# A decoder layer on one core: attention steps in another order, the last expert by hand, unread products

## The chip, the core and the metric

The kernel runs on one core of a Trainium2 chip. TensorE (PE) multiplies; its granted clock has two levels, 2.4 GHz (1.00 in the rows) and 1.2 GHz (0.50). VectorE (DVE), ScalarE (ACT) and GpSimd (POOL) work element by element; SyncE (SP) starts the loads of weights, one after the other. Sixteen DMA engines move the data. The metric is the device time of one launch in microseconds (us), the median of several runs. All times here are us unless marked ns.

## The reference

A decoder layer for S=256 tokens of D=1024, everything fp32: a condition c gives six vectors (shift, scale, gate, twice); attention with 16 heads of 64 (eight with compressed, selected and window branches, eight with a sliding window and a sink); a gated merge; an output projection; then 32 experts, of which each token uses four.

```python
mod = (cond @ w_ada + b_ada)                       # sh1, sc1, ga1, sh2, sc2, ga2
h = rms_norm(x, g_mix) * (1 + sc1) + sh1
q_n, kv_n, gate_n, q_s, kv_s, gate_m = split(h @ w_in)
o_n = nsa_attention(q_n, compress(k_c), compress(v_c), k_sl, v_sl, k_w, v_w, sigmoid(gate_n), rel_tab)
o_s = swa_attention(q_s, k_s, v_s, sinks, rel_tab)
g_a, g_b = split(sigmoid(gate_m))
x = x + ga1 * ((g_a * (o_n @ w_branch[0]) + g_b * (o_s @ w_branch[1])) @ w_out)
h = rms_norm(x, g_ffn) * (1 + sc2) + sh2
logits = h @ w_router + b_router                   # top 4 of 32, softmax over the four
for e in range(32):                                # each for the tokens that chose it
    y += gate_e * (clamped_swiglu(h @ w_up[e] + b_up[e]) @ w_down[e] + b_down[e])
return rms_norm(x + ga2 * y, g_final)
```

## The kernel before

**Weights.** All large weights come in chunks of 1 MB by `chunk()` (L197), which issues a load on SP's queue into one of 18 named slots (`ALL`), and into a nineteenth that the merge leaves. SP issues in program order: a load whose slot is not free holds up all behind it, and eight loads are under way at most. An expert is 12 chunks: 8 of `wup`, 4 of `wdn`. In the front of the program the same slots hold the chunks of w_ada, w_in, w_branch and w_out; as these are used up, the first chunks of experts 0 and 1 are loaded into them ahead of need.

**Front.** Products with fp32 weights are three products of a high and a low part: ACT casts the high part (L266), DVE subtracts for the low part (L271), and PE runs hh, hl and lh (L494 to L496, L990 to L992). `split` does both casts. The order of PE, DVE and ACT in the attention is written out by hand: classes `s0`, `s1` (sliding window) and `n0`, `n1` (the other eight heads) have steps `scores` (PE, then DVE L572 or L621 for bias and maximum, then ACT for the exponential L624), `weigh` (DVE and ACT L550, L552, each half of the heads times 1/sum), `turn` (PE transposes L538, ACT copies L540), `values` (PE L546) and `close` (ACT L523, DVE L524). `hidden` is the first layer of the compression (L771); its sum `hx` (L792) leaves its PSUM bank, for which the next piece of the merge gates waits. Between the steps `fill()` puts one piece of the merge gates on PE. After it come the branch products, `projected(q, f)` (w_out), and for each quarter q of the columns `added(q)` (residual), `turned(q)` (transposes, squares) and `logits(q)` (L1037).

**Choice of experts.** `fold` (L1077) adds the four partial logits, DVE finds the four best (L1080 to L1087), `pp` (L1090 to L1094) counts positions with products of 0/1 matrices, `oh` (L1139) is the one-hot matrix of expert 0's tokens. `gather` takes the norms of these tokens (L1129, fp32 products) and their rows in eight groups of 128 features (L1151, high and low part), DVE and ACT scale them to `XT` (L1153, L1154). Expert 0 starts with `z<-chunk,XT` (L1196): its first two columns of `XT` go through two banks each, so its first chunk is free after eight products.

**Last expert.** Its `wdn` is stored apart (`wlast`), four chunks of 256 columns each, the last in two parts of 0.5 MB. For each, PE multiplies (L1419), DVE scales (L1422), ACT and DVE split (L1427, L1428), PE spreads the rows back to the tokens (L1430, L1431), DVE adds to `y` (L1437), ACT squares (L1440). Then the last norm (L1444, L247) and the output in two halves of 512 columns for each 128 tokens (L1448 to L1451). The scheduler orders these engines.

Of the kernel before, what the change touches and what calls it, by code (L numbers as in the profile page):

```python
# [10 lines left out]
F32 = mybir.dt.float32  # L11
# [70 lines left out]
def _layout(inp):  # L82
# [40 lines left out]
    wl = wd[E - 1].reshape(2, 4, 128, 4, 256).transpose(3, 2, 1, 0, 4)  # L123
    tail = wl[3].reshape(128, 4, 2, 2, 128).transpose(0, 3, 1, 2, 4)
    out["wlast"] = c(np.concatenate([wl[:3].reshape(3, 128, 2048), tail.reshape(1, 128, 2048)]))
# [36 lines left out]
def tile_trunk(ctx: ExitStack, tc: tile.TileContext, A, out: bass.AP, dbg=None):  # L162
# [49 lines left out]
    count = fixed([1, E + 1], I32, "count")  # L212
    most = fixed([1, 1], F32, "most")
# [39 lines left out]
    with tc.tile_pool(name="front", bufs=1) as fr, tc.tile_pool(name="banks", bufs=1, space=PSUM) as ps:  # L253
# [54 lines left out]
        with tc.manual_schedule(engines=by_hand):  # L308
# [37 lines left out]
            ACT.copy(rrow, pr)  # L346

# [206 lines left out]
        class Sliding:  # L554
# [22 lines left out]
            def weigh(self):  # L577
                sm = self.sm
                V.tensor_tensor(sm[:, 2], sm[:, 0], C("sinks"), op=OP.add)
                ACT.activation(sm[:, 2], sm[:, 2], AF.Exp)  # L580
                V.tensor_tensor(sm[:, 1], sm[:, 1], sm[:, 2], op=OP.add)
                V.reciprocal(sm[:, 1], sm[:, 1])
                for i in range(4):
# [105 lines left out]
        with tc.manual_schedule(engines=by_hand):  # L689
# [24 lines left out]
            def compress(kv):  # L714
                kx = fr.tile([128, 2, S], F32, name="kx", tag="PT", bufs=4)
                for l2 in range(2):
                    for g in range(2):
                        eng = V.tensor_copy if g else ACT.copy
                        eng(kx[l2 * 64:l2 * 64 + 64, g, 0:S - l2], zb[0][g * 64:g * 64 + 64, kv, l2:S])
                b = bls[:, kv]  # L720
# [77 lines left out]
            ACT.activation(hu, hx, AF.Square)  # L798
            fill()
# [37 lines left out]
            n0.sums()  # L837
            n1.scores(0)
            n0.weigh(0)
# [16 lines left out]
            n0.values(1, pT)  # L856
            n1.scores(3)
            n0.compressed_turn()
# [31 lines left out]
            def branch_halves():  # L890
                for h in range(2):
                    for b in (1, 0):
                        w = chunk(A["wbr"], 2 * h + b).rearrange("p (f n) -> p f n", f=2)
                        for f in range(2):
                            yield split(w[:, f], 1024)
                ws = []
                for q, f in ((0, 0), (1, 0), (0, 1), (1, 1), (2, 0), (2, 1), (3, 0), (3, 1)):
                    if f == 0:
                        ws.append(chunk(A["wout"], q).rearrange("p (f n) -> p f n", f=2))
                    yield split(ws[q][:, f], 1024)  # L900
# [3 lines left out]
            nxt = next(ready)  # L904
            fill()

# [14 lines left out]
            for h in range(2):  # L921
                t = gm[h]
                for b in (1, 0):
                    pz = [bank(x, [128, 512]) for x in ("zo", "zz")[b]]
                    for f in range(2):
                        wh, wl = nxt
                        for i2 in range(2):
# [7 lines left out]
                            if i2 == 0:  # L935
                                nxt = next(ready)
                            elif f == 0:
                                next(passing)
# [35 lines left out]
            r2 = fixed([128, 2], F32, "r2")  # L974
            pl = bank("two", [128, S])
# [4 lines left out]
            def projected(q, f):  # L980
                wh, wl = nxt
                if f == 0:
                    pzs[q] = bank("z", [128, 2, 256])
                pz = pzs[q]
                for k4 in range(4):
# [7 lines left out]
                    if k4 == 1:  # L993
                        following = next(ready, None)
# [17 lines left out]
            def turned(q):  # L1012
                t, pt = tails[q]
                cs = slice(q * 256, q * 256 + 256)
                for d1 in range(2):
                    for a in range(2):
                        dk = 2 * q + d1
                        PE.transpose(pt[:, d1, a, :], xt[:, a, dk * 128:(dk + 1) * 128], ident)
                for k in range(2 * q, 2 * q + 2):
                    V.tensor_scalar(wr2[:, k], wr[:, k], G2[:, k:k + 1], None, op0=OP.mult)  # L1020
                for a in range(2):
                    ACT.activation(t[:, a], xt[:, a, cs], AF.Square, accum_out=ss[:, a, q:q + 1])
                if q == 3:
                    V.tensor_copy(x1T[:, 2 * q:2 * q + 2].rearrange("p a b -> p (a b)"), pt.rearrange("p a b c -> p (a b c)"))
                    V.tensor_reduce(s2, ss, X, OP.add)
                    V.tensor_scalar(s2, s2, 1.0 / D, 1e-5, op0=OP.mult, op1=OP.add)
                    root = POOL.tensor_tensor(r2, s2, half, op=OP.pow).ins
                else:
                    ACT.copy(x1T[:, 2 * q:2 * q + 2].rearrange("p a b -> p (a b)"), pt.rearrange("p a b c -> p (a b c)"))
# [9 lines left out]
            nxt = projected(0, 0)  # L1039
            merge_turn(1, 0)  # L1040
            next(passing)
            nxt = projected(1, 0)
            merge_turn(1, 1)
            nxt = projected(0, 1)
            next(passing)
            added(0)
            nxt = projected(1, 1)
            next(passing)
            added(1)
            turned(0)  # L1050
            nxt = projected(2, 0)
# [3 lines left out]
            nxt = projected(2, 1)  # L1055
# [5 lines left out]
            nxt = projected(3, 0)  # L1061
# [5 lines left out]
            logits(2)  # L1067
            added(3)
            turned(3)
            logits(3)  # L1070

# [22 lines left out]
        PE.matmul(pp[:, 2], ones, mask[:, 1], start=False, stop=True)  # L1094
        V.scalar_tensor_tensor(posm, pp[:, 0:2], 1.0, mask, op0=OP.add, op1=OP.mult)
        for name, t in (("d_x1", xt), ("d_lg", lg), ("d_posm", posm), ("d_gates", gates)):
# [19 lines left out]
    with tc.tile_pool(name="moe", bufs=1) as mo, tc.tile_pool(name="banks2", bufs=1, space=PSUM) as ps:  # L1116
# [7 lines left out]
        def norms(oh):  # L1124
# [3 lines left out]
            for a in range(2):  # L1128
                PE.matmul(p, r2[:, a:a + 1].to_broadcast([128, 128]), oh[:, a].bitcast(F32), start=a == 0, stop=a == 1)  # L1129
# [55 lines left out]
        def up(e, XT, c0, step=lambda j: None):  # L1185
# [3 lines left out]
            for n in range(2):  # L1189
                for j in range(4):  # L1190
                    if n == 0:
                        step(j)
                    w = chunk(A["wup"], e * 8 + 4 * n + j, slots=ALL).rearrange("p (k c f) -> p k c f", k=2, c=2)
                    for k in range(2):
                        for c in range(2):
                            PE.matmul(gu[n][64 * c:64 * c + 64], XT[:, 2 * j + k, c0:c0 + 64], w[:, k, c],  # L1196
                                      start=j == 0 and k == 0, stop=False)
                PE.matmul(gu[n], chosen[e % 2], bias[:, n * 512:(n + 1) * 512], start=False, stop=True)  # L1198
# [157 lines left out]
        with tc.issue_after(first[1]):  # L1356
            V.tensor_copy(count[:, 0:E], pp[0:1, 2])
            V.tensor_reduce(most, pp[0:1, 2], X, OP.max)
# [10 lines left out]
        for e in range(E):  # L1369
# [17 lines left out]
            if e == E - 1:  # L1387
                hT_ = [act(gu, n) for n in range(2)]
# [18 lines left out]
        ss = mo.tile([128, 2, 5], F32, name="ss3", tag="rr")  # L1407
        banks = pair("po") + pair("gu")
        for j in range(4):
            w = chunk(A["wlast"], j, slots=ALL, parts=1 + j // 3).rearrange("p (h b c n) -> p h c b n", h=1 + j // 3,  # L1410
                                                                             c=2, b=4)
            for h in range(1 + j // 3):
                n = 256 >> j // 3
                i = j + h
                cs = slice(j * 256 + h * n, j * 256 + h * n + n)
                po = (bank("pt", [128, 512]) if h else banks[j])[:, 0:n]
                for b in range(4):
                    for c in range(2):
                        PE.matmul(po[64 * c:64 * c + 64], hT_[b // 2][:, b % 2, 64 * c:64 * c + 64], w[:, h, c, b],  # L1419
                                  start=b == 0, stop=b == 3)  # L1420
                t = mo.tile([128, n], F32, name="t", tag="th", bufs=2)
                V.tensor_tensor(t, po, g2b[:, cs], op=OP.mult)  # L1422
                p = bank("s", [128, 2, 256])
                if j < 3:
                    hi = mo.tile([128, n], F32R, name="ohi")
                    lo = mo.tile([128, n], F32R, name="olo")
                    ACT.copy(hi, t)  # L1427
                    V.tensor_tensor(lo, t, hi.bitcast(F32), op=OP.subtract)  # L1428
                    for a in range(2):
                        PE.matmul(p[:, a], r[:, a], hi, start=a == 0, stop=False)  # L1430
                        PE.matmul(p[:, a], r[:, a], lo, start=False, stop=a == 1)  # L1431
                else:
                    p = [p[:, 0, 0:n], bank("s", [128, n])]
                    for a in range(2):
                        PE.matmul(p[a], r[:, a].bitcast(F32), t, start=True, stop=True)
                for a in range(2):
                    V.scalar_tensor_tensor(y[:, a, cs], p[a] if j == 3 else p[:, a], gates[:, a, E - 1:E], y[:, a, cs],  # L1437
                                           op0=OP.mult, op1=OP.add)
                    sq = mo.tile([128, n], F32, name="sq", tag="li")
                    ACT.activation(sq, y[:, a, cs], AF.Square, accum_out=ss[:, a, i:i + 1])  # L1440
                (V if h else POOL).tensor_tensor(last[:, :, cs], y[:, :, cs],
# [28 lines left out]
```

## Time and profile before

| what | value |
|---|---|
| median of 3 runs | 1182.69 (1178.37 to 1182.98) |
| profiled execution | 1183.18, of which 2.0 lie outside the span of 1181.2 |
| PE busy | 94% of the span |
| DVE, ACT busy | 43%, 23% |
| DMA | 463.61 MB, 392 GB/s in the mean |
| mean granted clock of PE | 0.977 |

Busy times are sums over the whole program. PE's share holds products that run while the weights of a later expert are still on their way, so a high share alone does not say that PE sets the end. A release "<-" in a row names what an engine's idle time ended with.

### The profile page before, as it was taken

To read this page: it belongs to the slowest core of one execution; us is meant where nothing else is said; L and a number is where in the kernel's file an instruction comes from. 1 tells how busy PE (TensorE), PEld (TensorE's weight loads), DVE (VectorE), ACT (ScalarE), POOL (GpSimd) and SP (SyncE) were. 2 spreads that over 40 slices of the span, in tenths; PEclk is the share of its full clock that TensorE was granted. 3 is DMA by queue.
4 is the path that set the end of the run, shared out by engine and by line. 5 is a ranking of instruction groups with operands and counts; after the bars stand their busy time and mean duration, and the time that the engine had idled before them with its cause. 6 is when DMAs were issued, how large, how long until landed. Compare 5 with 4: busy or idle time off the path is not lost. (4 is left out here: it accounts for less than half of the span.)

```text
span 1181.2 us, 13548 instructions
## 1 busy us (share of the span) xinstructions
PE 1106.8 (94%) x5209; PEld 488.8 (41%) x5210; DVE 513.3 (43%) x1067; ACT 266.1 (23%) x618; POOL 28.1 (2%) x25
## 2 busy tenths in 40 slices
PE   7998999899998999899999969999999999999996
PEld 6965678633342333223333324333333333333323
DVE  6877779623344323423343332333332333243333
ACT  4657734311120112111211112112111211121102
POOL 0000000100000000400000000000000000000001
PEclk9999999899999999999999989999999999999998
DMA  9986389899999999999999998999999999999995
GB/s 377 412 354 266 136 306 365 321 382 421 421 420 421 421 421 421 421 421 421 421 421 421 421 420 344 422 422 420 422 421 421 422 421 420 421 421 421 421 421 226
DMA packets 66598, 463.61 MB, mean 392 GB/s; under 512 B 7216, under 2 KB 9408, under 8 KB 11744
## 3 DMA queue, kind: packets, MB, share of 16 engines
q1 hardware_dynamic: 66048, 461.86, 95.1%
q8 instruction: 43, 0.70, 0.2%
q10 hardware_dynamic: 480, 0.83, 0.2%
q14 instruction: 27, 0.22, 0.0%
HBM read 461.59 MB, written 1.07 MB: 392 GB/s over the span
## 5 line engine op out<-in xcount | busy, mean ns | idle before, releaser
L1196 PE MATMUL z<-chunk,XT 128*64 128x512 f32 x2048 | 482.7, 602 | 1.5 <-DMA chunk<-in_wup 1.5
L1196 PEld LDWEIGHTS z<-chunk,XT 128*64 128x64 f32 x2048 | 136.4, 137 | 251.2 <-issue 238.7
L1242 PE MATMUL z<-chunk,hTe 128*64 128x512 f32 x496 | 135.4, 612 | 8.9 <-ACT hTe L1217 7.1
L1103 DVE TENSOR_SCALAR g<-z 128x256 f32<-128x256 f32 x64 | 27.1, 423 | 258.1 <-PE z L1198 258.1
L1242 PE MATMUL o<-chunk,hTe 128*64 128x512 f32 x496 | 132.3, 600 | 0.0
L1264 DVE SCALAR_TENSOR_TENSOR y<-s,gates,y 128x512 f32<-128x512 f32 x120 | 85.9, 746 | 70.8 <-PE s L1259 70.4
L1105 ACT ACTIVATE th<-g 128x256 f32<-128x256 f32 x64 | 26.6, 416 | 239.9 <-DVE g L1103 239.8
L1258 PE MATMUL s<-ohi,oht 128*128 128x512 f32 x124 | 55.7, 457 | 14.0 <-ACT ohi L1229 12.0
L1242 PEld LDWEIGHTS o<-chunk,hTe 128*64 128x64 f32 x496 | 36.9, 138 | 71.7 <-issue 71.7
L1229 ACT CAST ohi<-og 128x512 fp32r<-128x512 f32 x46 | 28.4, 618 | 151.0 <-DVE og L1228 151.0
L271 DVE TENSOR_TENSOR hilo<-chunk,hilo 128x1024 fp32r<-128x1024 f32 (+1 forms) x49 | 58.7, 1198 | 3.7 <-ACT hilo L266 3.7
L1228 DVE TENSOR_TENSOR og<-z,g2b 128x512 f32<-128x512 f32 x23 | 15.9, 691 | 97.2 <-PE z L1242 97.2
L1242 PEld LDWEIGHTS z<-chunk,hTe 128*64 128x64 f32 x496 | 31.4, 137 | 61.8 <-issue 45.7
L1217 ACT COPY hTe<-pt 128x256 f32<-128x256 f32 x64 | 23.8, 372 | 134.7 <-PE pt L1216 134.4
L1259 PE MATMUL s<-olo,oht 128*128 128x512 f32 x124 | 52.2, 430 | 0.2 <-DVE olo L1230 0.2
L1258 PEld LDWEIGHTS s<-ohi,oht 128*128 128x128 f32 x124 | 22.9, 188 | 69.2 <-ACT ohi L1229 29.0
L266 ACT CAST hilo<-chunk 128x1024 fp32r<-128x1024 f32 (+1 forms) x49 | 49.1, 1029 | 10.3 <-DMA chunk<-in_win 7.3
L1187 ACT CAST bias<-bias 128x128 fp32r<-128x128 f32 x32 | 9.4, 297 | 170.4 <-PE z L1198 167.4
L1230 DVE TENSOR_TENSOR olo<-og,ohi 128x512 fp32r<-128x512 f32 x46 | 31.8, 691 | 28.6 <-ACT ohi L1229 28.6
L1216 PE MATMUL pt<-kc,th 128*128 128x128 f32 x128 | 27.3, 292 | 10.0 <-DVE th L1109 7.0
L1216 PEld LDWEIGHTS pt<-kc,th 128*128 128x128 f32 x128 | 13.6, 141 | 52.4 <-DVE th L1109 18.0
L1182 DVE TENSOR_SCALAR oht<-pt,kc 128x256 fp32r<-128x256 f32 x32 | 15.4, 481 | 43.1 <-PE pt L1180 43.1
(338 smaller groups left out, 1277.1 us busy)
## 6 DMA issues: line engine op xcount, KB each, us to landing
chunk<-in_wup SPq DMA_DIRECT2D x256, 1024.0 KB, 19.8
chunk<-in_wdn SPq DMA_DIRECT2D x124, 1024.0 KB, 19.8
chunk<-in_wada SPq DMA_DIRECT2D x24, 1024.0 KB, 13.7
chunk<-in_wing SPq DMA_DIRECT2D x8, 1024.0 KB, 7.6
chunk<-in_win SPq DMA_DIRECT2D x7, 960.0 KB, 17.3
chunk<-in_w SPq DMA_DIRECT2D x4, 1024.0 KB, 15.0
chunk<-in_wbr SPq DMA_DIRECT2D x4, 1024.0 KB, 5.7
chunk<-in_wout SPq DMA_DIRECT2D x4, 1024.0 KB, 7.6
```

The source lines that it names most:

```text
L266: ACT.copy(t[:, 0, 0:n], src)
L271: V.tensor_tensor(t[:, 1, 0:n], src, t[:, 0, 0:n].bitcast(F32), op=OP.subtract)
L1103: V.tensor_scalar(g2, gu[:, 0:256], 7.0, 0.5, op0=OP.min, op1=OP.mult)
L1105: ACT.activation(t, g2, AF.Tanh, scale=1.702)
L1196: PE.matmul(gu[n][64 * c:64 * c + 64], XT[:, 2 * j + k, c0:c0 + 64], w[:, k, c], start=j == 0 and k == 0, stop=False)
L1216: PE.transpose(p[:, b], t[:, b * 128:(b + 1) * 128], ident)
L1229: ACT.copy(hi[:, n], o)
L1230: V.tensor_tensor(lo[:, n], o, hi[:, n].bitcast(F32), op=OP.subtract)
L1242: PE.matmul(po[n][64 * c:64 * c + 64], h[:, b, 64 * c:64 * c + 64], w[:, c, n * 512:(n + 1) * 512], start=n1 == 0 and b == 0, stop=n1 == 1 ...
L1258: PE.matmul(p, r[:, a], hi[:, n], start=True, stop=False)
L1259: PE.matmul(p, r[:, a], lo[:, n], start=False, stop=True)
L1264: V.scalar_tensor_tensor(ys, p, gates[:, a, e:e + 1], ys, op0=OP.mult, op1=OP.add)
```

## The change

It has six parts. (1) At the start four products that nobody reads go onto PE. (2) In the attention both copies of `compress` stand ahead of the position sums; `weigh` of the sliding heads is cut into `sinks`, `sums` and `weigh`, and `hx` and the weights stand ahead of `close`; `n0.weigh(0)` stands ahead of `n1.scores(0)`, and `compressed_turn` ahead of `n1.scores(3)`. (3) The high part of a w_branch or w_out chunk is cast a step before its low part. (4) In the choice of experts single products that nobody reads stand between PE's steps, six behind `fold` and two behind `pp`; the last `turned` copies its two halves on ACT and DVE; the norms of a gather take fp32r products of a high and a low part; the counts are read from a copy. (5) The last `wup` chunk's bias is added before the chunk. (6) The last expert's `wlast` is cut into two chunks of 512 columns (half of the inner sum each), one of 256 columns and two halves of 128; PE, DVE and ACT stand in an order written out by hand; the output goes out as 256 and 768 columns.

```diff
+    def idle(out, n):
+        for _ in range(n):
+            PE.matmul(out, ident, kc[:, 0:256], start=True, stop=True)
...
             ACT.copy(rrow, pr)
+            idle(pr, 4)
...
-            compress(0)
+            kxs = [compress(kv) for kv in range(2)]
             for a in range(2):
                 ACT.copy(vn[:, a], pv[a])
-            compress(1)
+            for kv in range(2):
+                positions(kv, kxs[kv])
...
             s1.scores(0)
+            s0.sinks()
+            s0.sums()
             s0.weigh()
             fill()
+            hidden(0)
             s1.scores(1)
-            hidden(0)
...
+            s1.sinks()
             ACT.copy(hx, ph[64:128])
+            s1.sums()
+            V.tensor_tensor(hx, ph[0:64], hx, op=OP.add)
             s1.weigh()
-            s0.close()
-            V.tensor_tensor(hx, ph[0:64], hx, op=OP.add)
             fill()
             T[0] = hankel(0)
             n0 = Selected(0)
             n0.scores(0)
             ACT.activation(hu, hx, AF.Square)
+            s0.close()
...
             n0.sums()
+            n0.weigh(0)
             n1.scores(0)
-            n0.weigh(0)
...
             n0.values(1, pT)
+            n0.compressed_turn()
             n1.scores(3)
-            n0.compressed_turn()
...
-                            yield split(w[:, f], 1024)
+                            yield high(w[:, f], 1024)
...
+            unread = bank("z", [128, 256])
+            idle(unread, 1)
+            scaled_router(3)
             added(3)
-            turned(3)
+            turned(3, unread)
             logits(3)
+            idle(unread, 1)
...
             fold = PE.matmul(pl[:, a], pls[:, a * 128:a * 128 + 128], K("fold"), start=True, stop=True).ins
+        with tc.issue_after(fold):
+            idle(unread, 6)
...
+        with tc.issue_after(summed_up):
+            idle(unread, 2)
...
-            for a in range(2):
-                PE.matmul(p, r2[:, a:a + 1].to_broadcast([128, 128]), oh[:, a].bitcast(F32), start=a == 0, stop=a == 1)
+            for j, (a, t) in enumerate(((0, r2h), (0, r2l), (1, r2h), (1, r2l))):
+                PE.matmul(p, t[:, a:a + 1].to_broadcast([128, 128]), oh[:, a], start=j == 0, stop=j == 3)
...
-            V.tensor_reduce(most, pp[0:1, 2], X, OP.max)
+            V.tensor_reduce(most, counted[0:1], X, OP.max)
...
+        cuts = [slice(0, 512), slice(512, 768), slice(768, 896), slice(896, 1024)]
...
+        with tc.manual_schedule(engines={PE.engine, V.engine, ACT.engine}):
...
+            V.tensor_reduce(sp, ss[:, :, 0:3], X, OP.add)
+            V.tensor_scalar(sp, sp, 1.0 / D, 1e-5, op0=OP.mult, op1=OP.add)
+            weighted(V, 2)
+            V.scalar_tensor_tensor(s3, ss[:, :, 3], 1.0 / D, sp, op0=OP.mult, op1=OP.add)
+            POOL.tensor_tensor(r3, s3, half, op=OP.pow)
+            weighted(V, 3)
+            for cs in (slice(0, 256), slice(256, 1024)):
```

PE from the last logits to the first product of expert 0, before (`L1037` logits, `L1018` transposes, `L1077` fold, `L1090` to `L1094` pp, `L1129` norms, `L1151` gather):

```order
L1037 MATMUL two<-x1T,router 32x256 x2
L1077 MATMUL o<-kc,pls 128x32 x2
L1090 LDWEIGHTS router
L1090 MATMUL o<-router 128x32
...
L1129 MATMUL s<-oh,r_1761 128x256 x2
L1151 MATMUL pt<-oh,xh 128x256 x2
L1151 MATMUL pt<-oh,xl 128x256 x2
...
L1196 MATMUL z<-chunk,XT 64x512 x4
L1151 MATMUL s<-oh,xh 128x256 x2
L1151 MATMUL s<-oh,xl 128x256 x2
L1196 MATMUL z<-chunk,XT 64x512 x3
```

The same place of the change (`L249` is the product that nobody reads, `L1123` fold, `L1138` to `L1142` pp, `L1181` norms, `L1203` gather, `L1250` expert 0):

```order
L1079 MATMUL two<-x1T,router 32x256 x2
L249 MATMUL z<-kc 128x256
L1123 MATMUL o<-kc,pls 128x32 x2
L249 MATMUL z<-kc 128x256 x6
L1138 LDWEIGHTS router
L1138 MATMUL o<-router 128x32
...
L249 MATMUL z<-kc 128x256 x2
L1181 MATMUL s<-oh,r2s 128x256 x2
...
L1250 MATMUL z<-chunk,XT 64x512 x4
L1203 MATMUL pt<-oh,xh 128x256 x2
L1203 MATMUL pt<-oh,xl 128x256 x2
L1250 MATMUL z<-chunk,XT 64x512 x4
```

PE has work in its order where it had none between `fold` and `pp` and between `pp` and the norms, and six groups of the gather stand ahead of expert 0 where five stood.

DVE where `hx` is computed in the attention, before (`L581`, `L582` sums, `L550` weigh of s1, `L524` close of s0, `L792` hx):

```order
L582 RECIPROCAL sw<-sw 128x8
L550 TENSOR_SCALAR Ps<-Ps,sw 128x256 x4
L524 SCALAR_TENSOR_TENSOR oTl<-o,oTh 128x4x128
L792 TENSOR_TENSOR hxu<-z,hxu 64x256
L461 SCALAR_TENSOR_TENSOR chunk,mod<-chunk,condrow 128x1024
```

The same place of the change (`L594` sums, `L813` hx, `L559` weigh):

```order
L594 RECIPROCAL sw<-sw 128x8
L813 TENSOR_TENSOR hxu<-z,hxu 64x256
L559 TENSOR_SCALAR Ps<-Ps,sw 128x256 x4
L470 SCALAR_TENSOR_TENSOR chunk,mod<-chunk,condrow 128x1024
L473 TENSOR_SCALAR G_66<-mod,cp 128x1
```

`hx` moved ahead of four weights and of the closing of s0.

## Rows read from the trace of the kernel before

**Rows 1.** Windows: busy time (count) of PE, PEld, DVE, ACT, POOL, clock, DMA share, GB/s.

```profile
14.00:16.00 2.00, 0.51 (x2) 0.31 (x2) 1.81 (x3) 1.71 (x3) 0.00 (x0) 1.00 1.00 415
160.00:216.00 56.00, 54.40 (x340) 47.30 (x339) 49.71 (x79) 24.88 (x41) 3.15 (x2) 1.00 0.91 355
250.00:700.00 450.00, 430.73 (x1859) 154.73 (x1855) 160.15 (x304) 62.10 (x143) 14.38 (x6) 0.99 1.01 421
```

**Rows 2.** The chain that ended last, in order of time: start, duration, what.

```profile
1137.44 19.80 DMA chunk<-in_wup
1157.29 1.94 PE z L1196 x8
```

**Rows 3.** SP's queue on the timeline, 195 to 245: first issue, length.

```profile
199.88 37.01 SPq L197 DMA_DIRECT2D chunk<-in_wup  x11
239.96 3.71 SPq L197 DMA_DIRECT2D chunk<-in_wdn  x3
```

**Rows 4.** What SP's queue waited for from 222 to 245: sum, times, longest.

```profile
SPq L197 <- PE z L1196: 14.0, 4, 8.4
```

**Rows 5.** Windows around the first weights of expert 0, columns as in the first group.

```profile
216.00:232.00 16.00, 10.10 (x56) 8.01 (x55) 7.83 (x32) 4.32 (x11) 3.21 (x3) 0.69 1.01 417
232.00:246.00 14.00, 14.00 (x68) 5.75 (x68) 5.97 (x19) 3.64 (x11) 0.00 (x0) 0.99 0.62 226
```

**Rows 6.** PE on the timeline, 232 to 241.

```profile
232.91 1.94 PE L1196 MATMUL z<-chunk,XT 128*64 128x512 f32 x8
235.44 1.93 PE L1196 MATMUL z<-chunk,XT 128*64 128x512 f32 x6
```

**Rows 7.** What PE waited for from 56 to 245: sum, times, longest.

```profile
PE z L494 <- DVE hxu L792: 2.4, 1, 2.4
PE o L1090 <- DVE router L1087: 2.4, 1, 2.4
PE s L1129 <- DVE bias L1360: 1.4, 1, 1.4
PE pt L538 <- ACT P L552: 1.4, 1, 1.4
PE o L684 <- ACT pcT L679: 0.9, 1, 0.9
PE z L933 <- DVE hilo L271: 0.8, 1, 0.8
```

**Rows 8.** Windows where the clock is low, columns as in the first group.

```profile
94.00:100.00 6.00, 5.77 (x23) 4.32 (x24) 5.41 (x25) 4.70 (x18) 0.00 (x0) 0.72 1.02 425
116.00:124.00 8.00, 8.00 (x26) 4.54 (x26) 5.21 (x18) 4.58 (x16) 0.00 (x0) 0.57 0.35 131
222.00:232.00 10.00, 6.15 (x27) 5.61 (x28) 4.58 (x23) 2.90 (x6) 1.12 (x1) 0.50 1.02 424
```

**Rows 9.** ACT on the timeline of the attention.

```profile
124.39 1.07 ACT L540 COPY PT<-pt 128x512 f32<-128x512 f32 x2 [2.46 <-PE pt L538]
```

**Rows 10.** PE, DVE and ACT on the timeline, choice of experts to first gather.

```profile
222.06 1.06 PE L1077 MATMUL o<-kc,pls 128*128 128x32 f32 x4 [0.53 <-DVE pls L1074]
...
225.24 0.22 DVE L1087 TENSOR_TENSOR router<-router 128x64 bf16<-128x64 f32 x1
...
226.11 0.76 DVE L1139 TENSOR_TENSOR oh<-kc,posm 128x256 fp32r<-128x256 f32 x2
...
227.21 2.04 PE L1129 MATMUL s<-oh,r 128*128 128x256 f32 x4 [1.39 <-DVE bias L1360]
...
229.90 0.63 PE L1151 MATMUL s<-oh,xh 128*128 128x256 f32 x2
```

**Rows 11.** Timeline of the last expert's end.

```profile
1159.69 0.42 DVE L1103 TENSOR_SCALAR g<-z 128x256 f32<-128x256 f32 x1 [7.50 <-PE z L1198]
...
1174.45 0.16 DVE L1444 TENSOR_REDUCE s<-ss 128x2 f32<-128x10 f32 x1 [0.20 <-ACT sq L1440]
...
1176.38 0.96 ACTq L1451 DMA_DIRECT2D out<-last  x2
```

More of the change, by code (lines that the diff above doesn't have):

```diff
@@ L211, in tile_trunk @@
     gates = fixed([128, 2, E], F32, "gates")
-    count = fixed([1, E + 1], I32, "count")
-    most = fixed([1, 1], F32, "most")
+    count = fixed([1, E + 2], I32, "count")
+    most = count[:, E + 1:E + 2].bitcast(F32)
     half = fixed([128, 2], F32, "half")
@@ L899, in branch_halves @@
                         ws.append(chunk(A["wout"], q).rearrange("p (f n) -> p f n", f=2))
-                    yield split(ws[q][:, f], 1024)
+                    yield high(ws[q][:, f], 1024)
             ready = branch_halves()
             fill(PIECES - filled[0] - 1)
-            nxt = next(ready)
+            nxt = low(*next(ready))
             fill()
+            coming = next(ready)
             def merged(h):
@@ L935, in tile_trunk @@
                             if i2 == 0:
-                                nxt = next(ready)
-                            elif f == 0:
-                                next(passing)
+                                nxt = low(*coming)
+                            else:
+                                coming = next(ready)
+                                if f == 0:
+                                    next(passing)
                         if h and b and f == 0:
@@ L992, in projected @@
                         PE.matmul(pz[:, a], mTl[:, k, ta], wh[:, ws], start=False, stop=k == 7 and a == 1)
-                    if k4 == 1:
-                        following = next(ready, None)
+                    if k4 == 1 and coming:
+                        following = low(*coming), next(ready, None)
                 return following
@@ L1067, in tile_trunk @@
             logits(2)
+            unread = bank("z", [128, 256])
+            idle(unread, 1)
+            scaled_router(3)
             added(3)
-            turned(3)
+            turned(3, unread)
             logits(3)
+            idle(unread, 1)
         pls = fr.tile([128, S], F32, name="pls", tag="PT", bufs=4)
@@ L1093, in tile_trunk @@
         PE.matmul(pp[:, 2], ones, mask[:, 0], start=True, stop=False)
-        PE.matmul(pp[:, 2], ones, mask[:, 1], start=False, stop=True)
+        summed_up = PE.matmul(pp[:, 2], ones, mask[:, 1], start=False, stop=True).ins
+        with tc.issue_after(summed_up):
+            idle(unread, 2)
         V.scalar_tensor_tensor(posm, pp[:, 0:2], 1.0, mask, op0=OP.add, op1=OP.mult)
+        counted = part([E])
+        ACT.copy(counted[0:1], pp[0:1, 2])
         for name, t in (("d_x1", xt), ("d_lg", lg), ("d_posm", posm), ("d_gates", gates)):
@@ L1192, in up @@
                         step(j)
+                    if j == 3 and e == E - 1:
+                        PE.matmul(gu[n], chosen[e % 2], bias[:, n * 512:(n + 1) * 512], start=False, stop=False)
                     w = chunk(A["wup"], e * 8 + 4 * n + j, slots=ALL).rearrange("p (k c f) -> p k c f", k=2, c=2)
@@ L1406, in tile_trunk @@
         last = fixed([128, 2, D], F32, "last", "XT")
[L1407 to L1441, printed above, removed]
-                                                 gfb[:, None, cs].to_broadcast([128, 2, n]), op=OP.mult)
@@ L1443, in tile_trunk @@
-        s3 = mo.tile([128, 2], F32, name="s3", tag="pe")
-        V.tensor_reduce(s3, ss, X, OP.add)
-        r3 = pow_half(mo, s3, "r3", "ge")
-        for n in range(2):
-            cs = slice(n * 512, n * 512 + 512)
-            V.tensor_scalar(last[:, 0, cs], last[:, 0, cs], r3[:, 0:1], None, op0=OP.mult)
-            nc.sync.dma_start(out[0:128, cs], last[:, 0, cs])
-            ACT.mul(last[:, 1, cs], last[:, 1, cs], r3[:, 1:2])
-            nc.scalar.dma_start(out[128:256, cs], last[:, 1, cs])
+        ss = mo.tile([128, 2, 4], F32, name="ss3", tag="rr")
@@ new lines, in tile_trunk, with product @@
+        s3 = mo.tile([128, 2], F32, name="s3", tag="pe")
+        sp = mo.tile([128, 2], F32, name="sp", tag="ge")
+        hT_ = [act(gu, 0)]
+        cuts = [slice(0, 512), slice(512, 768), slice(768, 896), slice(896, 1024)]
+        sums = [bank(t, [128, 512]) for t in ("z", "o")]
+        def product(i, w, bs, first=True, final=True):
+            for b in bs:
+                for c in range(2):
+                    PE.matmul(sums[i][64 * c:64 * c + 64, 0:cuts[i].stop - cuts[i].start],
+                              hT_[b // 2][:, b % 2, 64 * c:64 * c + 64], w[:, c, b - bs[0]],
+                              start=first and b == bs[0], stop=final and b == bs[-1])
```

142 lines of the change are left out of this document (119 added, 23 removed).

## Prediction, on record before the changed kernel ran

> **What bounds the kernel now.** I read the windows of the whole program first. In the two long expert stretches DMA is at a share of 1.01 and 421 GB/s, while PE's busy time also reads 96% [rows 1]. Which of the two leads is told by the chain that ended last: before the last up chunk it holds nothing but loads of 19.8 us, and PE's eight records at 1157.29 start when the load behind 1137.44 ends [rows 2]. A chunk of 1 MB takes 1.05 MB / 421 GB/s = 2.49, so an expert's twelve take 29.9. So in this stretch time is bytes over 421 GB/s, and an engine that works faster inside it brings nothing. The end moves by three things: when the stream of weights can start and run unbroken, gaps in it, and what follows its last byte.
>
> The start is seen on SP's queue. Eleven loads stand under one row from 199.88, the last of them at 236.6, the next row starts at 239.96 [rows 3]; the longest wait in them, 8.4, is for expert 0's own products [rows 4]. All slots are full and the stream stops until PE has used up a chunk. From 216 to 232 DMA still runs at 417 GB/s, from 232 to 246 only at 226 [rows 5]: 14 x (1 - 226/421) = 6.5 us of stream are lost there. PE starts expert 0 at 232.91, leaves it for a group of the gather, and comes back at 235.44 [rows 6]; the second pair of products there, 0.86 later, ends the use of the first chunk, at 236.3. So the front is worth its time one to one: whatever brings expert 0 forward brings the whole stream forward, as long as the loads ahead of it are in by then. They have room: from 160 to 216 DMA moves 355 GB/s, 56 x (1 - 355/421) = 8.8 us below its rate [rows 1].
>
> In the front PE waits for DVE and ACT. The list of waits from 56 to 245 has few long ones [rows 7], and behind the long ones the clock reads 0.50 for some us [rows 8].
>
> **The change part by part.**
>
> *Products at the start* (1): nothing. They stand where PE is busy for 0.51 of 2 us while DVE and ACT, which split the weights, have 1.81 and 1.71 [rows 1]: DVE covers them. Four take 4 x 0.43 = 1.7 (below) at the high clock; without the cover that would be their cost.
>
> *Attention* (2). The bound from above is all the waits that it can take away: 2.4 (`hx`), 1.4 (`P`), 0.9 (`pcT`), 4.7 together [rows 7], and what the low clock costs behind the first two. PE is busy nearly all of the stretches behind them, so each loses its length times what the mean clock lacks: 6 x (1 - 0.72) = 1.7 behind `hx`, 8 x (1 - 0.57) = 3.4 behind `P` [rows 8]. That makes 9.8. Not all goes. With `hx` ahead of `weigh` and `close`, the next piece of the gates no longer waits for it, but then for ACT's sigmoid of the piece before, about 1.0. ACT stands idle where PE is late, as for 2.46 before 124.39 [rows 9]; with PE earlier, ACT's four exponentials and four weights become the later ones, and I work out by hand a new wait of about 2.3 for `weigh` of n1 near 119. Following both orders by the durations of before, PE stands 3 to 4 us earlier where it now waits for `pcT`. I take 3.5, with 0 and 8 as ends.
>
> *Casts a step earlier* (3), and `added` ahead of the merge's passing. From 160 to 216 PE is busy 54.40 of 56 [rows 1], so 1.6 is all there is, half of it the wait for `hilo` [rows 7]. The high cast then never waits for PE's step; I take 1.0. Attention and casts together: 4.5 (1.5 to 8).
>
> *Choice of experts* (4). `fold` ends in a falling clock, then PE waits 2.4 for the mask and 1.4 before the norms [rows 7], and from there the gather runs at 0.50: two products take 0.21 each there (0.63 with the tail of the second), norms 2.04 [rows 10]. Six unread products behind `fold` are fp32 of 256 columns; the nearest row is the norms', two such products in 2.04 at the low clock with the tail in it, so about 0.85 each, 0.43 at the high one. If the clock holds, six end 2.6 behind `fold`, at 225.15, while the mask ends at about 225.0 (225.24 + 0.22 before [rows 10], less 0.5 because `fold` ends earlier): `pp` is not delayed. Mask, `posm` and `oh` (0.76) then put the norms at 226.5 instead of 227.21, four one-pass products at 0.107 in place of 2.04, and the gather at 0.107 a product: six groups of four are 2.6, where five groups took 4.2. Expert 0 starts at 229.5 instead of 232.91. Its first chunk is free after 1.72 + 0.43 + 0.86 more, at 232.5 instead of 236.3, and the second slot at 233.4, where the second issue stood at 239.96 [rows 3]. The stream, which ran out at about 232.5, then loses some 1.5 in place of 6.5: a gain of 5.0. The most is 6.5. If the clock stays at 0.50 in spite of the products, the six take 5.1, end at 227.7, and delay `pp` from 225.52 by 2.1 or so; less the cheaper norms (1.2) and with the other savings that is between +1.2 and -2.
>
> One rule bears on this. From 222 to 232 the granted clock is 0.50 and PE busy for 6.15 of 10 us [rows 8]; before that it was busy for 10.10 - 6.15 = 3.95 of the 6 us from 216 [rows 5, 8], and the whole gather pays for it. The Trainium skill, page "TensorE: Matmul & The Clock Gate", section "What's actually happening", says that the throttled state is the default and activity lifts it, but also that for modelling the ramp costs under 1% of a typical kernel's span and that the count of slow products varies from run to run. By that the products would be left out of the sum, and a run could fall into the low clock in spite of them; the sum would be the one of the second rival. The rows put a price on one place, so I go by them.
>
> *Bias early and the last expert* (5, 6). From the last bias product to the sum of squares the timeline takes from 1159.69 to 1174.45, and the last output is issued at 1176.38 [rows 11]. With the bias ahead of the last chunk, swiglu starts about 0.5 earlier. After the last byte, DVE and ACT work through what the scheduler left in a queue; in the new order the larger pieces come first, the mean of the first three is made before the last square, and half the columns of the first two chunks are multiplied before hT is complete. By hand, with the durations of before, the sum of squares is ready 1.35 earlier; the first output piece is 256 columns instead of 512, which brings the first issue forward by a few tenths. I take 1.5 (0.5 to 2.5). There is no cover for a loss here: all after the last byte is on the path.
>
> The sum: 4.5 + 5.0 + 1.5 = 11.0. The profiled execution took 1183.18, so 1172.2, close to its median's 1171.7; I say **1172**.
>
> **The rivals.**
>
> *The attention's waits only move* (chance 0.14). ACT and DVE have nearly as much to do there as PE's own path, and each step needs the others'. If the new wait at `weigh` of n1 is longer than the 1.4 it replaces, the clock falls again and the gain shrinks to about 1: 1183.18 - 1 - 5.0 - 1.5 = 1175.7. For it speaks that the order moves work and removes none; against it that `hx` needs 0.41 of DVE and waited behind four weights and a close.
>
> *The clock is not held in the choice of experts* (0.14). Single products of 0.43 with gaps between are little work. Then 4.5 + 1.2 + 1.5 give 1176.0, and with `pp` delayed, 4.5 - 2 + 1.5 give 1179.2. The skill's rule named above would have this outcome.
>
> *The loads hold expert 0 instead* (0.08): if the slots come free no earlier, the stream ends filling at 232.5 as before and the front's 4.5 buys only the rest of the gap: at most 6.5 - 0.5 + 1.5 = 7.5, 1175.7. DMA at 417 GB/s just before 232 [rows 5] speaks for it, the 8.8 us of room before 216 against it.
>
> *Nothing reaches the end* (0.07): gains of one place are waited away in the next; about 1182.
>
> *Slower* (0.05). One mechanism in the attention: n0's weights stand ahead of n1's scores on DVE and ACT, and so the exponentials that `turn` needs come later. A wait of PE of 1.4 was followed by the low clock, 3.4 lost [rows 7, 8]: with 2.3 for the wait, a new one costs 5.7. From 6.5 lost in the front on (5.0 + 1.5) the kernel is not faster; at three such waits beyond those removed, 1183.18 + 17.1 - 6.5 = 1193.8. The attention of before has two waits of 1.4 or more [rows 7]; this needs five, with the same work in it.
>
> **How the numbers follow.** My forecast has a chance of 0.52; its own range is 1168.5 to 1176. To leave out no more than 2 in 10, the range reaches down to the upper ends of the terms (8 + 6.5 + 2.5 gives 1166, and a little beyond, since low ends are also my guesses) and up over the clock rival's 1179.2: 1164.5 to 1180.5. A change of 0.5%, 5.9 us, is about what a measurement of this kernel can tell from none; faster than 1176.8 holds nearly all of the forecast and some six in ten of the first three rivals, 0.73; slower than 1188.6, 0.04.
>
> **What would show it.** Right: the row of 232 to 246 above 370 GB/s; the clock 1.00 from 222 to 232; expert 0's first product at 225 or so (229.5 less 4.5); no wait for `hx` over 1.2; the last load landing 9 to 10 earlier; 22 us from there to the end instead of 24. Wrong: the clock at 0.50 in the gather although products stand in the gaps; a new wait near 119 with a low clock behind it; SP's longest wait still at expert 0's products; the tail unchanged.

## The result and the profile after

The changed kernel takes 1173.34 (1173.2 to 1173.42, 4 runs), the kernel before 1182.84 (1178.37 to 1183.53, 4 runs): a ratio of 0.9935, 95% interval 0.9906 to 0.9964. The forecast was 1172, with a range of 1164.5 to 1180.5. The kernel before does not repeat itself as the changed one does: measured three more times beside the experiments, its medians were 1179.12 (29 runs), 1178.58 (19) and 1179.3 (8), with single runs from 1176.77 to 1183.87; where that comes from is the first experiment.

Against the profiled execution of before (span 1181.2), that of after has a span of 1171.5, 9.7 less. It divides into three parts: the front, the pause of the weight stream, and the end. DVE's first instruction of the last `added` and PE's first product of expert 0, on the timeline of after (207 to 236):

```profile
213.75 0.42 DVE L1037 TENSOR_TENSOR t<-z,g1b 128x256 f32<-128x256 f32 x1 [2.40 <-PE z L1021]
...
218.11 2.84 PE L249 MATMUL z<-kc 128*128 128x256 f32 x12
220.54 0.22 DVE L1135 TENSOR_TENSOR router<-router 128x64 bf16<-128x64 f32 x1
220.82 0.18 PE L1138 MATMUL o<-router 128*128 128x32 bf16 x1
...
225.52 1.94 PE L1250 MATMUL z<-chunk,XT 128*64 128x512 f32 x8
229.18 0.33 SPq L199 DMA_DIRECT2D chunk<-in_wup  x1
```

`added` stood at 217.96 before: the front is 4.2 shorter. The six unread products (twelve records) start at 218.11, and the position products at 220.82, 0.28 after the last step of their mask starts, the same as before (225.24 [rows 10] and 225.52): they are not held up. Expert 0 starts 7.4 earlier than at 232.91 [rows 6], and the load that waits for its first chunk is issued at 229.18 instead of 236.56, the last of the eleven in [rows 3].

Windows of the changed kernel, columns as in [rows 1]:

```profile
90.00:100.00 10.00, 9.20 (x50) 5.56 (x48) 7.61 (x30) 8.18 (x26) 0.00 (x0) 1.00 1.01 422
110.00:120.00 10.00, 8.62 (x45) 5.06 (x45) 9.27 (x33) 9.10 (x30) 0.00 (x0) 1.00 0.59 211
222.00:232.00 10.00, 9.89 (x60) 5.67 (x59) 6.09 (x23) 4.55 (x14) 0.00 (x0) 1.00 0.83 324
232.00:246.00 14.00, 13.21 (x57) 4.60 (x57) 4.76 (x12) 1.90 (x5) 0.00 (x0) 1.00 1.01 421
```

The clock is 1.00 where it was low [rows 8]. The stream still stops, now between 222 and 232: 10 x (1 - 324/421) = 2.3 in place of 6.5 [rows 5], 4.2 gained. PE's last up chunk and the end, from the same timeline (1145 to 1172):

```profile
1148.94 1.94 PE L1250 MATMUL z<-chunk,XT 128*64 128x512 f32 x8
...
1164.91 0.16 DVE L1555 SCALAR_TENSOR_TENSOR s<-ss,sp 128x2 f32<-128x2 f32 x1 [0.18 <-ACT sq L1504]
```

From the last up chunk to the end it is 1171.5 - 1148.9 = 22.6, where it was 1181.2 - 1157.3 = 23.9 [rows 2]: 1.3. So 4.2 + 4.2 + 1.3 = 9.7. The last up chunk is in 8.4 earlier (1157.3 to 1148.9), where the prediction looked for 9 to 10.

What PE waits for from 56 to 245, in the changed kernel (sum, times, longest):

```profile
PE z L1020 <- DVE hilo L278: 1.6, 3, 0.7
PE pt L547 <- DVE kb L864: 1.3, 1, 1.3
PE o L555 <- ACT PT L549: 0.9, 1, 0.9
PE z L1297 <- ACT hTe L1272: 0.8, 1, 0.8
PE z L957 <- DVE hilo L278: 0.7, 1, 0.7
```

The waits for `hx`, `P`, `pcT`, the mask and the norms [rows 7] are gone. In their place stand 1.3 for `kb` ahead of the first `turn`, 0.9 for a copy, and 1.6 for the low casts of w_out, which was 0.2 before. The wait for `hilo` in the branch products stays, 0.7 (L957) where it was 0.8 (L933 [rows 7]).

### The profile page after: what moved, and what is told of

Same layout as the page of the kernel before. It is cut to its first block, busy times and chain, and to the rows that moved or that the text cites. A ratio compares the mean times of both kernels' runs of the same rounds, so it can differ in the third digit from the quotient of the medians.

```text
span 1171.5 us, 13567 instructions
## 1 busy us (share of the span) xinstructions
PE 1103.6 (94%) x5221; PEld 483.5 (41%) x5222; DVE 512.0 (44%) x1065; ACT 265.4 (23%) x616; POOL 27.7 (2%) x25
## 5 line engine op out<-in xcount | busy, mean ns | idle before, releaser
L1250 PE MATMUL z<-chunk,XT 128*64 128x512 f32 x2048 | 484.7, 602 | 1.0 <-DMA chunk<-in_wup 0.8
L1250 PEld LDWEIGHTS z<-chunk,XT 128*64 128x64 f32 x2048 | 136.0, 137 | 250.1 <-issue 237.4
L1205 DVE SCALAR_TENSOR_TENSOR XT<-pt,G,rr 128x256 f32<-128x256 f32 x32 | 15.3, 480 | 44.0 <-PE z L1250 34.0
## 6 DMA issues: line engine op xcount, KB each, us to landing
chunk<-in_win SPq DMA_DIRECT2D x7, 960.0 KB, 17.2
```

What stands on the lines that cost most here:

```text
L1205: done = V.scalar_tensor_tensor(XT[:, d], p, G2[:, d:d + 1], rr, op0=OP.mult, op1=OP.mult).ins
```

## The experiments

**The kernel before, profiled twice more**, with no edit.

> The kernel before, unchanged, looked at once more, since its executions lie in three groups near 1177, 1178.7 and 1183. If the groups are the low clock in the attention: an execution near 1177 has clock 1.00 from 90 to 130 and its last added starts at 213.5, as in the run with only unread products; one near 1178.7 has the low clock behind hx alone, 215.4; one near 1183 both, 218. If the groups come from elsewhere (the loads, the choice of experts): the last added starts at 218 in all of them.

> The same as the run before it, once more: last added at 213.5, 215.4 or 218 with the time of its group, 1177, 1178.7 or 1183, if the clock in the attention makes the groups; 218 in all of them if not.

Measured: 1182.81 and 1177.74. What PE waits for is the same in both to a tenth, 2.4 for `hx` and 1.4 for `P`. Windows of the first, then of the second:

```profile
94.00:100.00 6.00, 6.00 (x24) 4.27 (x24) 5.24 (x24) 4.52 (x18) 0.00 (x0) 0.72 1.02 423
116.00:124.00 8.00, 8.00 (x28) 4.68 (x29) 4.89 (x18) 4.26 (x15) 0.00 (x0) 0.61 0.37 131
222.00:232.00 10.00, 6.21 (x31) 5.65 (x32) 4.87 (x22) 2.94 (x6) 0.82 (x1) 0.52 1.00 417
232.00:246.00 14.00, 14.00 (x67) 5.41 (x67) 5.66 (x19) 3.62 (x10) 0.00 (x0) 1.00 0.61 227
```

```profile
94.00:100.00 6.00, 5.39 (x28) 3.53 (x28) 5.80 (x26) 5.17 (x19) 0.00 (x0) 1.00 1.02 425
116.00:124.00 8.00, 8.00 (x40) 4.38 (x40) 6.42 (x28) 6.44 (x23) 0.00 (x0) 1.00 0.28 116
222.00:232.00 10.00, 9.48 (x42) 6.12 (x42) 6.00 (x22) 4.44 (x13) 0.00 (x0) 0.79 0.64 270
232.00:246.00 14.00, 14.00 (x64) 5.22 (x64) 3.30 (x9) 1.44 (x4) 0.00 (x0) 1.00 0.93 365
```

Three places of the front, on the timelines of the first, of the second and of the changed kernel: DVE's first scaled queries (`qn`), PE's first product that takes `pcT`, and the last `added` (for the changed kernel shown above, 213.75):

```profile
58.96 0.41 DVE L430 TENSOR_SCALAR qn<-z 128x256 f32<-128x256 f32 x1
...
132.59 1.16 PE L684 MATMUL o<-pcT,G 128*128 128x128 f32 x8 [0.88 <-ACT pcT L679]
...
217.65 0.42 DVE L1008 TENSOR_TENSOR t<-z,g1b 128x256 f32<-128x256 f32 x1 [2.75 <-PE z L992]
```

```profile
59.69 0.41 DVE L430 TENSOR_SCALAR qn<-z 128x256 f32<-128x256 f32 x1
...
128.63 1.16 PE L684 MATMUL o<-pcT,G 128*128 128x128 f32 x8 [0.86 <-ACT pcT L679]
...
213.69 0.42 DVE L1008 TENSOR_TENSOR t<-z,g1b 128x256 f32<-128x256 f32 x1 [2.75 <-PE z L992]
```

```profile
59.21 0.41 DVE L439 TENSOR_SCALAR qn<-z 128x256 f32<-128x256 f32 x1
...
127.58 1.05 PE L699 MATMUL o<-pcT,G 128*128 128x128 f32 x8
```

The same program with the same waits, but in one execution the clock falls behind both and in the other behind neither; that makes 4.0 at the last `added`. So the expectation holds for the two groups seen. The group near 1178.7 was not caught in a profile. The second execution reaches the last `added` as early as the changed kernel (213.75).

The three places divide the front. From the queries to `pcT` the first execution takes 73.6, the second 68.9 and the changed kernel 68.4: the low clock costs 4.7 there, and the new order by itself gains 0.6. From `pcT` to the last `added` it is 85.1 in both executions of before and 86.2 in the changed kernel, which loses 1.1 there; part 3 of the change lies in this stretch. Up to the queries the second execution is 0.7 later than the first: near 50 ACT waits 1.19 for PE in it, and 0.19 in the first, and its clock from 16 to 22 reads 0.55 against 0.72.

**The old attention order in the changed kernel**, all other edits left.

```diff
             s1.scores(0)
-            s0.sinks()
-            s0.sums()
             s0.weigh()
...
-            n0.weigh(0)
             n1.scores(0)
+            n0.weigh(0)
```

> The changed kernel with the attention in the order of before (casts, choice of experts and tail stay changed). If the order is worth what was predicted: the waits for hx and P come back with the low clock behind them, the last added starts 3.5 to 4.5 later than 213.75, time 1173.3 + 4 = 1177.3. If the waits only moved and the front's gain came from the casts: 1173.3 to 1174.3.

Measured: 1175.32 (1173.52 to 1178.22), 10 runs. In the profiled one, at 1174.93, the clock falls behind `hx` only:

```profile
90.00:100.00 10.00, 7.60 (x34) 5.08 (x34) 8.13 (x31) 8.61 (x26) 0.00 (x0) 0.83 1.01 422
110.00:120.00 10.00, 8.61 (x42) 5.14 (x41) 9.73 (x40) 8.17 (x27) 0.00 (x0) 1.00 0.64 211
...
215.44 0.42 DVE L1023 TENSOR_TENSOR t<-z,g1b 128x256 f32<-128x256 f32 x1 [2.40 <-PE z L1007]
```

2.0 in the median, half of what was expected, and a spread of 4.7 where the changed kernel has 0.2. From the queries to `pcT` it takes 70.4. The next kernel takes the clock out of it.

**The same with unread products in its two waits.**

```diff
             V.tensor_tensor(hx, ph[0:64], hx, op=OP.add)
+            idle(bank("pt", [128, 256]), 5)
             fill()
...
             fill(2)
+            idle(bank("pt", [128, 256]), 3)
             pT = n0.turn(0)
```

> The changed kernel with the attention in the order of before and eight unread products in its two long waits (five ahead of the gates' piece that waits for hx, three ahead of the first turn). If the order of before costs only through the low clock behind its waits: clock 1.00 from 90 to 130, the last added starts at 213.5 to 214, the time is that of the changed kernel, 1173.3 to 1173.8, and no execution stands 2 or 3 above the others. If the waits themselves cost, as half of the predicted term says: 1175 or more, as without the products (1175.3).

Measured: 1174.49 (1174.0 to 1176.08), 9 runs. Windows and the last `added` of an execution at 1176.08:

```profile
90.00:100.00 10.00, 9.73 (x51) 6.52 (x50) 8.48 (x32) 8.86 (x28) 0.00 (x0) 1.00 1.01 417
110.00:120.00 10.00, 8.93 (x49) 5.80 (x47) 9.16 (x32) 8.88 (x29) 0.00 (x0) 1.00 0.58 210
...
214.59 0.42 DVE L1025 TENSOR_TENSOR t<-z,g1b 128x256 f32<-128x256 f32 x1 [2.40 <-PE z L1009]
```

With the clock held throughout, the last `added` stands 0.84 later than the changed one's 213.75. From the queries to `pcT` it takes 69.4 here, 1.1 more than the changed kernel, and 68.9 in the unfilled execution of before that kept its clock; the filling itself seems to take the 0.5 between them. So the order by itself is worth 0.6, not the 3.5 of the prediction; neither expectation hits the number, since the waits do cost, but little. The rest of this execution's 1176.08 lies behind 246 and was not followed up.

**Both casts in one step again**, with `added` behind the merge's passing.

```diff
-                            nxt = low(*coming)
+                            nxt = next(ready)
...
-                        following = low(*coming), next(ready, None)
+                        following = next(ready, None)
```

> The changed kernel with both casts of a weight in one step again, and the order of added and passing as before. If the casts are worth the 1.0 of the prediction: PE waits 0.7 to 0.8 for hilo near 180, the last added starts 0.5 to 1 later than 213.75, time 1174.3. If PE only waits elsewhere for the same DVE work: 1173.3.

Measured: 1172.31 (1172.17 to 1172.71), 4 runs, ratio to before 0.9955 (0.9939 to 0.9972); faster than the changed kernel by 1.0. Its waits of PE from 160 to 216, and its last `added`:

```profile
PE z L956 <- DVE hilo L278: 0.7, 1, 0.7
PE two L1075 <- DVE router L1039: 0.5, 1, 0.5
PE z L1016 <- DVE hilo L278: 0.2, 1, 0.2
...
212.75 0.42 DVE L1033 TENSOR_TENSOR t<-z,g1b 128x256 f32<-128x256 f32 x1 [2.40 <-PE z L1017]
```

The 1.6 for w_out's low casts is 0.2 again, and the last `added` stands 1.0 earlier; from `pcT` to it the kernel takes 85.1, as before the change. Part 3 of the change loses what it was to gain. Which half does it, the casts or the place of `added`, was not tried apart.

**No unread products in the choice of experts.** The eleven are taken out, the four at the start stay.

```diff
-        with tc.issue_after(fold):
-            idle(unread, 6)
...
-        with tc.issue_after(summed_up):
-            idle(unread, 2)
```

> The changed kernel without the eleven unread products in the choice of experts (the four at the start stay). If they matter because they hold the clock: the granted clock falls to 0.50 from about 218 on, the gather runs at half rate, the first product of expert 0 comes 2.5 to 4 later than 225.5, the stream's pause grows from 2.3 to 5 or 6, and the time is 1173.3 + 3 to 4 = 1176 to 1177. If the clock falls or holds whatever stands there, or costs too little to see, and the other edits of this place made the gain: within 0.7 of 1173.3.

Measured: 1175.54 (1174.63 to 1176.54), 10 runs. Windows:

```profile
222.00:232.00 10.00, 10.00 (x46) 6.60 (x46) 5.60 (x18) 4.29 (x13) 0.00 (x0) 0.76 0.65 261
232.00:246.00 14.00, 13.95 (x60) 4.50 (x56) 2.83 (x8) 1.50 (x4) 0.00 (x0) 1.00 0.95 375
```

The clock falls in the gather (0.76), expert 0 starts at 226.83 with its last `added` at 213.22, 13.6 later, where the changed kernel needs 11.8. The pause is 3.8 + 1.5 = 5.3. The mechanism is the expected one; its price is 2.2, below the 3 to 4 expected, since here the clock is low for a part of the stretch only.

**Nothing but these products in the kernel before.**

```diff
             logits(2)
+            unread = bank("z", [128, 256])
+            idle(unread, 1)
             added(3)
...
+        with tc.issue_after(fold):
+            idle(unread, 6)
```

> The kernel before with nothing but the eleven unread products in the choice of experts added at the same places. If the clock is what they bring: clock 1.00 from 222 to 232, expert 0 starts about 2.5 earlier than 232.9, the pause of the stream shrinks from 6.5 to about 3.5, time 1182.8 - 3 = 1179.8. If they stand in the way of the position products, or change nothing: 1182.8 or more.

Measured: 1176.18 (1175.82 to 1176.9), 10 runs; before 1179.12 beside it, ratio 0.9971 (0.9956 to 0.9986). Windows, and the last `added`:

```profile
222.00:232.00 10.00, 9.57 (x55) 5.80 (x56) 6.16 (x23) 4.70 (x14) 0.00 (x0) 1.00 0.71 286
232.00:246.00 14.00, 13.54 (x63) 5.17 (x61) 4.66 (x12) 1.91 (x5) 0.00 (x0) 1.00 0.99 406
...
213.52 0.42 DVE L1013 TENSOR_TENSOR t<-z,g1b 128x256 f32<-128x256 f32 x1 [2.75 <-PE z L997]
```

2.9 of the 3 expected, but against a median that mixes executions with the low clock in the attention and without. In the profiled one, at 1175.88, the attention kept its clock; against the execution of before that kept it too (1177.74) it is 1.9, and the pause is 3.2 + 0.5 = 3.7 against 5.5. All ten runs lie within 1.1; why this kernel, whose attention is the one of before, never fell to 1180 or more in ten runs is open.

**Twelve unread products behind the fold in place of six.**

```diff
-            idle(unread, 6)
+            idle(unread, 12)
```

> The changed kernel with twelve in place of six unread products behind the fold. If expert 0 sets the stream one to one: the six more take 2.6 of PE, the position products start at 223.3 in place of 220.8, all behind them 2.4 later, the pause of the stream grows from 2.3 to 4.7, time 1175.7. If the stream has slack there: 1173.3 to 1173.8.

Measured: 1175.67 (1175.42 to 1176.0), 10 runs. Expert 0 starts at 228.06, and the windows read

```profile
222.00:232.00 10.00, 9.89 (x64) 6.66 (x62) 6.93 (x25) 4.73 (x15) 0.00 (x0) 1.00 0.64 268
232.00:246.00 14.00, 14.00 (x61) 4.83 (x58) 2.86 (x8) 0.97 (x3) 0.00 (x0) 1.00 0.93 383
```

A delay of 2.5 at expert 0 is 2.3 at the end, and the pause is 3.6 + 1.3 = 4.9. The front counts one to one, as the prediction has it.

**The old end of the last expert.** `wlast`, its loop and the bias as before.

```diff
-        cuts = [slice(0, 512), slice(512, 768), slice(768, 896), slice(896, 1024)]
+        for j in range(4):
+            w = chunk(A["wlast"], j, slots=ALL, parts=1 + j // 3).rearrange("p (h b c n) -> p h c b n", h=1 + j // 3,
```

> The changed kernel with the last expert's end as before (four chunks of 256 columns, bias behind the last chunk, output in halves). If the new end is worth what the traces say: the last chunk of the up weights lands at the same time, 1148.9, and 23.9 in place of 22.6 follow it, time 1174.6 to 1174.8. If the end only looks shorter because the stream in front of it differs: 1173.3.

Measured: 1174.39 (1174.17 to 1174.78), 8 runs. Timeline:

```profile
1148.45 1.94 PE L1246 MATMUL z<-chunk,XT 128*64 128x512 f32 x8 [0.44 <-DMA chunk<-in_wup]
...
1165.63 0.16 DVE L1494 TENSOR_REDUCE s<-ss 128x2 f32<-128x10 f32 x1 [0.19 <-ACT sq L1490]
```

From the last up chunk to the sum of squares it takes 17.2, in the changed kernel 1164.91 - 1148.94 = 16.0: 1.2; in the runs 1.05.

**No unread products at the start.**

```diff
             ACT.copy(rrow, pr)
-            idle(pr, 4)
```

> The changed kernel without the four unread products at the start. If DVE and ACT cover them, as predicted: within 0.4 of 1173.3, though the clock from 16 to 22 falls to 0.50 again as before. If the start's low clock reaches the end: 1174.5 or more.

Measured: 1173.52 (1172.79 to 1173.86), 5 runs. In time they bring nothing that these runs can tell: 0.2 within a spread of 1.1. The trace tells more:

```profile
20.22 0.41 PE L313 MATMUL two<-hl,hilo 128*128 128x256 f32 x1
20.43 0.41 PE L311 MATMUL two<-hh,hilo 128*128 128x256 f32 x1
...
50.06 0.94 ACT L273 CAST hilo<-chunk 128x896 fp32r<-128x896 f32 x1 [0.87 <-PE pt L406]
```

The row of the window 16 to 22 reads 1.00, but PE's products stand 0.21 apart in it until 20.85, and 0.12 from there on, as they do from 16.4 on in the changed kernel. So without the four products the clock was low there, as expected, and the row does not show it. DVE and ACT do not cover it fully: ACT waits 0.87 for PE near 50, where the changed kernel waits 0.31. In this execution DVE came to the same instruction near 35 by 0.6 earlier (34.84 instead of 35.40), which hides the loss.

**Two edits against what is left.** Expert 0 finishes its first chunk first:

```diff
+                    with tc.issue_after(opened[0]) if e == 0 and n == 1 and j == 0 else nullcontext():
                         for k in range(2):
```

> The changed kernel, in which expert 0 finishes its first chunk (its own four products) before it starts the first chunk of the other half. If the pause of the stream is the wait for that chunk: it comes free about 1.3 earlier than 228.9, the pause shrinks from 2.3 to about 1.2, time 1173.3 - 1.1 = 1172.2. If the second release then becomes what the stream waits for: 1173.3, within 0.3.

Measured: 1173.0 (1172.41 to 1173.24), 5 runs. Windows:

```profile
222.00:232.00 10.00, 10.00 (x59) 5.58 (x59) 5.89 (x22) 4.45 (x14) 0.00 (x0) 1.00 0.88 354
232.00:246.00 14.00, 13.21 (x57) 4.62 (x57) 4.76 (x12) 1.90 (x5) 0.00 (x0) 1.00 0.98 393
```

The pause moves: 1.6 before 232 and 0.9 behind it, 2.5 in all. The first waiting load goes out earlier, the second only at 229.82 (230.04 in the changed kernel): the second waits now, as the rival in the expectation said. And with the casts of before as well:

> Both edits that were faster than the changed kernel together: casts in one step as before, and expert 0 finishing its first chunk first. If they act in two places, the front 1.0 and the pause 0.3 to 0.5: 1171.8 to 1172.0. If the earlier front only meets slots that still fill: 1172.3, as with the casts alone.

Measured: 1172.11 (1172.07 to 1172.76), 4 runs, ratio to before 0.9934 (0.9909 to 0.996): 1.2 under the changed kernel and the fastest here, but within 0.2 of the casts alone.

## Why the prediction was right, and where not

The sum was 11.0 and the traces show 9.7; 1172 was forecast and 1173.34 measured. By the steps of the prediction:

- **What bounds it** held: a delay or a gain at expert 0 goes to the end one to one (twelve products: 2.5 there, 2.3 at the end). The rival that the loads hold expert 0 fell.
- **Attention and casts**, 4.5 forecast, 4.2 in the two profiles. The size is right, the make-up is not, and that is luck: about 5.2 of gain and 1.1 of loss, and an execution of before with the low clock at both waits to measure against.
- **Attention**, 3.5 forecast. The step that failed is "PE stands 3 to 4 us earlier where it now waits for `pcT`", which takes the low clock for a fixed price of the waits. Counted from the queries, PE stands 5.2 earlier there against an execution with the low clock at both waits (73.6 to 68.4) and 0.6 against one without (68.9). The price of the low clock, 1.7 + 3.4, was nearly right: 4.7. What was wrong is that it comes with the waits: two executions of before with the same waits lie 4.0 apart at the last `added`. The new wait of about 2.3 near 119 did not come either; the longest in the attention is the 1.3 for `kb`.
- **Casts**, 1.0 forecast as a gain: a loss of 1.1 in the trace, 1.0 when undone. "The high cast then never waits for PE's step" missed that PE waits for the low cast, which is DVE's: 0.7 of the 0.8 for `hilo` stayed, and 1.6 for w_out's low casts came on top. Why DVE is later with them was not followed.
- **Choice of experts**, 5.0 forecast, 4.2 measured in the pause. The clock was held, `pp` was not delayed, expert 0 starts 11.8 behind the last `added` where 11.5 was worked out (229.5 - 217.96), and its first chunk is free 3.4 behind that start (229.18 less the 0.3 of the issue, less 225.52) where 3.0 was; these two are 0.6 of the 0.8 by which the forecast of the pause, 1.5, was too low. The products that hold the clock and the cheaper norms with the new order of the gather can be told apart by the pauses at held clock in the attention: 5.5 with neither (before at 1177.74), 5.3 without the products, 3.7 with nothing but the products, 2.3 with both. So the products bring 1.8 alone and 3.0 beside the other edits, and the other edits 0.2 alone and 1.4 beside the products: the two help each other. The remaining 1.0 of the 4.2 is again the execution measured against, whose pause was 6.5. All these are single profiles; in the runs, taking the products out costs 2.2.
- **The end**, 1.5 forecast, 1.3 in the traces and 1.05 when undone. **The start**, nothing forecast: 0.2 within a spread of 1.1 in the runs. That DVE and ACT cover a low clock there holds for the profiled execution of before; where the clock is low for longer, as in the run without the four products and in the second execution of before, some 0.7 gets past them by 59.
- **What was added up against.** The profiled execution of before was one with the clock low at both waits. Against the one at 1177.74 the front gives nothing and the change is worth 4.4: a pause of 3.6 + 1.9 = 5.5 that becomes 2.3, and 1.3 at the end. The forecast's 11 was for the kind with the low clock, and the four runs that it is compared with were, by their times, mostly of that kind; against the medians of the later measurements the change is worth 5 to 6. The rest of the 9.5 is which executions of before were met. The changed attention kept its clock in all eight profiles that have it.

## What to carry to other kernels

Before a wait is priced by the low clock behind it, look at a second execution: the wait repeats, the clock need not. Where a stream of weights runs at its rate, price an edit at the place at which the stream stops, and check which release comes next. Each product here needs a high and a low cast: before one of them is moved, see which of the two PE waits for.

## What the runs showed of the hardware

The granted clock fell or held behind the same waits of 2.4 and 1.4 in executions of the same program: 0.72 and 0.61 in the run at 1182.81, 1.00 and 1.00 in the one at 1177.74. The Trainium skill, page "TensorE: Matmul & The Clock Gate", section "What's actually happening", says of the start of a kernel that the count of slow products varies from run to run. At the start these runs agree (0.72 and 0.55 from 16 to 22 in the same two executions), and they show the same in the middle of a kernel, of which that passage does not speak. The same section puts the ramp under 1% of a typical kernel's span: here one execution lost 5.1 of 1182.8 against another, with the low clock as the only difference seen, 0.4%, which is inside that figure and still more than half of the 9.5 between the two kernels.

In the changed kernel PE waits 1.3 for `kb` ahead of the first `turn`, about as long as for `P` before, and the window around it reads 1.00; its four runs lie within 0.2, so it did not fall there in any of them by as much as it did before.
